# First mixer: two latent projections and the query projection interleaved with the gate projections

## The chip, the cores and the metric

The kernel runs on one core of a Trainium2 chip as one launch. The metric is the device time of that launch in microseconds (us); lower is better. Engines are named as in the profile: PE is TensorE (matmuls), PEld its weight loads, DVE is VectorE, ACT is ScalarE, POOL is GpSimd, SP issues the weight transfers.

## The reference, cut to what matters

Three blocks of a transformer (one hybrid block, then two layers with other mixers) run over 256 tokens of width 1024 in float32. The change lies in the mixer of the first block. With `h` the normalised input (256 x 1024):

```
z = h @ w_in                       # split: q_lat 256, c_kv 128 + k_pe 32, qb 512, kb 128, vb 128, gate_a 1024, gate_b 1024
cq   = rmsnorm(q_lat);  qa  = cq   @ w_qb    # 8 heads x (64 + 32), rope on the 32
c_kv = rmsnorm(c_kv);   kva = c_kv @ w_kvb   # 8 heads x (64 keys + 64 values)
oa = softmax(qa . [ka, rope(k_pe)]) va       # attention A, 8 heads
ob = softmax(rope(norm(qb)) . rope(norm(kb))) vb   # attention B, 8 query heads on 2 key heads
x += (sigmoid(gate_a) * (oa @ w_oa) + sigmoid(gate_b) * (ob @ w_ob)) @ w_o
```

So attention A needs the three short products of `cq` and `c_kv` (here: the latent projections), attention B does not, and the gates are needed only behind both.

## The kernel before, in words

**Tiles.** Activations lie transposed, features on the 128 partitions and the 256 tokens along the free dimension. Each operand is split in a high and a low part, and a product is three matmuls (`mm3`, L323 to L326: high weights times high and low activations, low weights times high ones). `gemm_a` (L328) makes two 128-column tiles of an output per PSUM bank of the tag `acc`, of which there are three, used in turn; `gemm_b` (L367) keeps tokens as rows and takes two of these banks. An `acc` bank is free again once DVE or ACT has read it.

**Weights.** All weights come through one stream, in the order in which they are used, 128 x 1024 floats per chunk. `Stream.prep` (L135) lets ACT make the rounded high part (L140), `Stream.low` (L145) lets DVE make the low part one chunk behind (L149), and this orders the next transfer on SP (L131). Eight 128-column pieces use up one chunk.

**Order.** Nothing is reordered by a planner: each engine runs its instructions in the order in which the Python code emits them. The emission is a round robin written out by hand (`Sched`): a projection is a generator that yields once per 128-column piece, that is per three matmuls; this is a **step** below. After each step every side task counts down and emits its next part when its count is over. Step 0 is here the first step after the query projection of attention B. `done` of a `gemm_a` tile pair is called as the next step begins, so the read of its bank stands in the queues ahead of that step's side tasks.

**The stretch in question.** Before: steps 0 to 3 are `kn` (4 pieces of w_kvb, keys of A, two banks, each read by two ACT copies, L861), steps 4 and 5 are `va` (gemm_b, one 512-column piece, matmuls at L374 to L376, banks read by ACT L864 and DVE L865), steps 6 to 21 are the query projection (w_qb, 8 tiles of 2 pieces, four banks, each read by a DVE multiplication with the rope table, L873), and steps 22 to 149 are the eight gate pairs (16 pieces each; a bank is read by DVE L887 and then ACT L888). Behind step 149, `drain` emits what attention still has, and then `gemm_merge` (matmuls of `oh`, `ol`) begins, first with the output of attention A.

Side tasks in this stretch, by their counts in the code: keys of B are transposed and scaled after step 16 (L711, DVE L713, ACT L714) and their low part made after step 19 (L716); a bias table for a much later mixer is made after step 19 (PE L546, ACT L548, an ACT-issued write to DRAM L549 and an ACT-issued broadcast L550 that reads it back); `attn1` (L766) takes B as soon as its keys and queries are there, in both kernels after step 20, and then moves one head every 6 steps: scores (PE L400 for B, L777 for A, bank tag `wk`, three banks), row maximum (DVE L791), exponential (ACT L797), transposes (PE L804, DVE L806), product with the values (PE L816). Head 8, the first of A, waits for the flag `qa`, which `ev_qa` sets after the fourth query bank:

```
while not all(z in st for z in need):
    yield 1
pr[i] = soft(*units[i])
```

Five steps after the last product of a half, `final` transposes the outputs (PE L831) and splits them into `oh` (ACT L406) and `ol` (DVE L407).

Of the kernel before, what the change touches and what calls it, by code (L numbers as in the profile page):

```python
# [217 lines left out]
def build(ctx, tc, nc, aps, total, stop=None):  # L218
# [22 lines left out]
    sc = Sched()  # L241
# [46 lines left out]
    def C(name, r=slice(0, P)):  # L288
        o, w = CST[name]
        if o >= NC1:  # L290
            return rope[0][r, o - NC1:o - NC1 + w]
        return cst[r, o:o + w]
# [18 lines left out]
    def t512():  # L311
        return tmp.tile([P, 512], F32, name="t512", bufs=7)
# [4 lines left out]
    def v2(ap):  # L317
        return ap.rearrange("p (a b) -> p a b", a=2)

    def bc(ap, n):  # L320
        return ap[:, None, :].to_broadcast([ap.shape[0], n, ap.shape[1]])

    def mm3(o, ah, al, bh, bl, start, stop_, joint=False):  # L323
        PE.matmul(o, ah, bh, start=start, stop=False, skip_group_check=joint)  # L324
        PE.matmul(o, ah, bl, start=False, stop=False, skip_group_check=joint)  # L325
        PE.matmul(o, al, bh, start=False, stop=stop_, skip_group_check=joint)  # L326

    def gemm_a(n, K, piece, rhs, done, M=P, lead=0, width=2, order=None, ready=None, joint=False):  # L328

        order = order or list(range(K))

        def part(t, ps, j, k0, k1):
            m = M(t) if callable(M) else M
            for k in order[k0:k1]:
                while ready and not ready(k):
                    yield
                wh, wl = W.get(piece(t, k), m)
                xh, xl = rhs(k)  # L340
                mm3(ps[:m, j * T:(j + 1) * T], wh, wl, xh, xl, k == order[0] and not (joint and j), k == order[-1], joint)
                yield

        i = 0
        if lead:
            banks = [(t, accb()) for t in range(0, 2 * width, 2)]
            i = 2 * width
            cuts = (0,) + (lead if isinstance(lead, tuple) else (lead,)) + (K,)
            for k0, k1 in zip(cuts, cuts[1:]):
                for t, ps in banks:  # L350
                    for j in range(1 + joint):
                        yield from part(t + j, ps, j, k0, k1)
                    if joint and k1 == K:
                        done(t // 2, ps)
            for t, ps in banks:
                if not joint:
                    yield from part(t + 1, ps, 1, 0, K)
                    done(t // 2, ps)
            joint = False
        while i < n:  # L360
            ps = accb()
            for j in range(min(2, n - i)):
                yield from part(i + j, ps, j, 0, K)
            done(i // 2, ps)
            i += 2

    def gemm_b(N, K, piece, lhs, done, tail=0, each=None):  # L367

        o = accb(), accb()

        def step(k, b, w):
            xh, xl = lhs(k)
            s = slice(b * P, (b + 1) * P)
            PE.matmul(o[b][:, :N], xh[:, s], w[0], start=(k == 0), stop=False)  # L374
            PE.matmul(o[b][:, :N], xl[:, s], w[0], start=False, stop=False)  # L375
            PE.matmul(o[b][:, :N], xh[:, s], w[1], start=False, stop=(k == K - 1))  # L376

        for k in range(K - tail):
            w = W.get(piece(k), N)
            for b in range(2):  # L380
                step(k, b, w)
                yield
        w = [W.get(piece(k), N) for k in range(K - tail, K)]
        for b in range(2):
            for j in range(tail):
                step(K - tail + j, b, w[j])
                yield
            if each:
                each(b, o[b])
        if done:  # L390
            done(o)
# [10 lines left out]
    def rhs_of(h, l):  # L402
        return lambda k: (h[:, k], l[:, k])
# [80 lines left out]
    hrhs = rhs_of(hx, lx)  # L484
# [5 lines left out]
    def later(n, fn):  # L490
        def g():
            yield n
            fn()
        sc.side(g())

    def idx(a, n):
        return list(range(a, a + n))
# [76 lines left out]
    ckh = mp.tile([P, T], F32R, name="ckh")  # L574
    ckl = mp.tile([P, T], F32R, name="ckl")
    cqh = mp.tile([P, 2, T], F32R, name="cqh")
    cql = mp.tile([P, 2, T], F32R, name="cql")
# [20 lines left out]
    def w_in_piece(tiles):  # L598
        return lambda t, k: ("w_in", k, tiles[t])
# [263 lines left out]
    def ev_va(p):  # L863
        S_.copy(vA[:, 0], p[0])  # L864
        V.tensor_copy(vA[:, 1], p[1])  # L865

    def qa_cols(h):
        b = h * 96
        return idx(b, 64) + idx(b + 64, 32) + idx(b + 80, 16) + idx(b + 64, 16)

    def ev_qa(i, ps):
        def go():
            V.tensor_tensor(QA[:, 2 * i:2 * i + 2], v2(ps), bc(C("tq"), 2), op=OP.mult)  # L873
            if i == 3:
                later(4, lambda: st.update(qa=True))
        sc.push(go)

    def latents():
        yield from gemm_a(4, 1, lambda t, k: ("w_kvb", 0, idx(t * 256, 64) + idx(t * 256 + 128, 64)), lambda k: (ckh, ckl), ev_kn)
        yield from gemm_b(512, 1, lambda k: ("w_kvb", 0, [h * 128 + 64 + j for h in range(8) for j in range(64)]),  # L880
                          lambda k: (ckh, ckl), lambda p: sc.push(lambda: ev_va(p)))
        yield from gemm_a(8, 2, lambda t, k: ("w_qb", k, qa_cols(t)), rhs_of(cqh, cql), ev_qa)

    def ev_gate(i, ps):
        def go():
            t = t512()
            V.tensor_tensor(v2(t), v2(ps), bc(n1.row, 2), op=OP.mult)  # L887
            S_.activation(sg[:, 2 * i:2 * i + 2], v2(t), AF.Tanh, scale=0.5)  # L888
        sc.push(go)

    gt = [idx(IN["ga"] + 128 * i, 128) for i in range(16)]

    sc.run(latents())
    sc.run(gemm_a(16, 8, w_in_piece(gt), hrhs, ev_gate))
    sc.flush()
    sc.drain(lambda: "o11" in st)

# [911 lines left out]
def make(arr, total, stop=None):  # L1809
    import concourse.bacc as bacc  # L1810

    nc = bacc.Bacc("TRN2", target_bir_lowering=False, num_devices=1, dynamic_dma_scratch_size=4096)
    aps = {n: nc.dram_tensor(n, v.shape, mybir.dt.from_np(v.dtype), kind="ExternalInput").ap() for n, v in arr.items()}
    aps["w"] = nc.dram_tensor("w", (total * P,), F32, kind="ExternalInput").ap()
    aps["out"] = nc.dram_tensor("out", (P, KD, T) if stop else (T, D), F32, kind="ExternalOutput").ap()
    with tile.TileContext(nc) as tc, ExitStack() as ctx:
        W = build(ctx, tc, nc, aps, total, stop)
    return nc, W
# [11 lines left out]
```

## Time and profile before

| | us |
|---|---|
| three runs, median | 1387.05 |
| lowest and highest of them | 1381.07, 1394.16 |
| profiled execution, its own time | 1386.93 |
| its span from first to last instruction | 1385.2 |
| PE busy in the span | 1360.4 (98%) |
| DVE busy | 909.1 (66%) |
| ACT busy | 689.0 (50%) |

The stretch from step 0 to step 149 lies at 40.6 to 141.8 us of the span. [...] In the chain of work that ended last PE holds 93% of the span and DVE 3%.

### The profile page before, as it was taken

How to read it: one execution, taken by the hardware profiler on the slowest of the kernel's cores; microseconds unless marked ns; L12 is line 12 of the kernel's file. 1: busy time of each engine (PE TensorE's matmuls, PEld its weight loads, DVE VectorE, ACT ScalarE, POOL GpSimd, SP SyncE). 2: the span in 40 equal slices, each digit the busy share in tenths (PEclk: the TensorE clock that was granted, in tenths of full speed). 3: DMA queues.
4: the chain of work that ended last, by engine and by line, in shares of the span. 5: the costliest groups of instructions: out<-in, count | busy, mean ns of one | idle time of the engine just before them, and what ended most of it. 6: DMA issues, size and time to landing. Idle time of an engine off the chain costs nothing.

```text
span 1385.2 us, 27163 instructions
## 1 busy us (share of the span) xinstructions
PE 1360.4 (98%) x11342; PEld 1333.0 (96%) x11342; DVE 909.1 (66%) x1254; ACT 689.0 (50%) x970; POOL 103.1 (7%) x108
## 2 busy tenths in 40 slices
PE   9899999999999999999999999999999999999998
PEld 8799999999999999997999999999999988999987
DVE  6866776656687665675865555655656777776553
ACT  6554465544554544453554444444444364544442
POOL 2300000000040000010000000000000271000001
PEclk9899999999999999999999999999999999999999
DMA  8533555665646656552455555555555532555552
GB/s 279 187 127 97 190 191 188 198 198 183 198 155 218 192 185 207 191 180 66 153 192 189 185 186 189 173 187 189 190 194 186 196 107 92 167 191 191 189 177 84
DMA packets 69642, 243.61 MB, mean 176 GB/s; under 512 B 7877, under 2 KB 11365, under 8 KB 69392
## 3 DMA queue, kind: packets, MB, share of 16 engines
q1 hardware_dynamic: 66096, 234.52, 51.6%
q10 hardware_dynamic: 2992, 5.99, 1.3%
q8 instruction: 89, 1.46, 0.4%
q0 software_dynamic: 432, 1.37, 0.3%
q14 instruction: 33, 0.27, 0.1%
HBM read 240.78 MB, written 4.22 MB: 177 GB/s over the span
## 4 chain that ended last, share of the span: by engine, by line
PE 93%; DVE 3%; issue 1%; DMA 1%; ACT 1%; POOL 1%; SPq 0%; POOLq 0%; DVEq 0%; ACTq 0%
PE acc L324 27%; PE acc L326 26%; PE acc L325 26%; PE acc L374 2%; PE acc L376 2%; PE acc L375 2%; PE pv L816 1%; PE wk L400 1%; DVE wlo L149 1%; DMA wraw<-w 1%; DVE iacc L1621 1%; PE wk L1212 1%; PE wk L804 1%; PE wk L777 0%; POOL rs_y L415 0%
## 5 line engine op out<-in xcount | busy, mean ns | idle before, releaser
L149 DVE TENSOR_TENSOR wlo<-wraw,whi 128x1024 fp32r<-128x1024 f32 (+2 forms) x442 | 533.2, 1220 | 248.5 <-PE acc L326 187.9
L140 ACT CAST whi<-wraw 128x1024 fp32r<-128x1024 f32 (+1 forms) x448 | 462.1, 1038 | 362.4 <-PE acc L325 261.5
L324 PE MATMUL acc<-hx,whi 128*128 128x256 f32 x2184 | 621.9, 285 | 0.2 <-ACT hx L410 0.2
L325 PE MATMUL acc<-lx,whi 128*128 128x256 f32 x2184 | 610.5, 280 | 1.4 <-DVE lx L411 1.4
L326 PE MATMUL acc<-hx,wlo 128*128 128x256 f32 x2184 | 610.7, 280 | 0.4 <-DVE wlo L149 0.4
L325 PEld LDWEIGHTS acc<-lx,whi 128*128 128x128 f32 x2184 | 412.9, 189 | 2.1 <-DVE lx L411 1.7
L326 PEld LDWEIGHTS acc<-hx,wlo 128*128 128x128 f32 x2184 | 413.3, 189 | 0.9 <-DVE wlo L149 0.9
L324 PEld LDWEIGHTS acc<-hx,whi 128*128 128x128 f32 x2184 | 410.8, 188 | 3.0 <-issue 0.6
L324 PE MATMUL acc<-gh,whi 128*128 128x256 f32 x784 | 218.1, 278 | 0.0
L325 PE MATMUL acc<-gl,whi 128*128 128x256 f32 x784 | 218.1, 278 | 0.0
L326 PE MATMUL acc<-gh,wlo 128*128 128x256 f32 x784 | 218.1, 278 | 0.0
L326 PEld LDWEIGHTS acc<-gh,wlo 128*128 128x128 f32 x784 | 147.9, 189 | 0.0
L325 PEld LDWEIGHTS acc<-gl,whi 128*128 128x128 f32 x784 | 147.9, 189 | 0.0
L324 PEld LDWEIGHTS acc<-gh,whi 128*128 128x128 f32 x784 | 147.2, 188 | 0.0
L415 POOL TENSOR_TENSOR rs_y<-col,mhalf 128x2 f32<-128x2 f32 (+2 forms) x17 | 19.1, 1124 | 823.8 <-DVE col L443 757.2
L407 DVE TENSOR_TENSOR gl<-t,gh 128x512 fp32r<-128x512 f32 x60 | 41.5, 692 | 41.4 <-ACT gh L406 41.4
L406 ACT CAST gh<-t 128x512 fp32r<-128x512 f32 x60 | 37.3, 622 | 45.7 <-DVE t L1086 33.3
L410 ACT ACTIVATE hx<-x,gains 128x256 fp32r<-128x256 f32 x64 | 29.5, 502 | 54.9 <-DVE x L482 48.8
L324 PE MATMUL acc<-oh,whi 128*128 128x256 f32 x192 | 54.8, 285 | 0.0
L325 PE MATMUL acc<-ol,whi 128*128 128x256 f32 x192 | 53.6, 279 | 0.0
L326 PE MATMUL acc<-oh,wlo 128*128 128x256 f32 x192 | 53.6, 279 | 0.0
L1086 DVE TENSOR_TENSOR t<-t,acc 128x512 f32<-128x512 f32 x44 | 30.3, 689 | 32.4 <-ACT t L1084 26.8
(383 smaller groups left out, 1478.9 us busy)
## 6 DMA issues: line engine op xcount, KB each, us to landing
wraw<-w SPq DMA_DIRECT2D x439, 512.0 KB, 4.2
t5r<-t5u ACTq DMA_DIRECT2D x1, 3072.0 KB, 12.0
Bt<-t5r ACTq DMA_DIRECT2D x1, 2048.0 KB, 11.9
wraw<-w SPq DMA_DIRECT2D x7, 256.0 KB, 4.7
x<-xt SPq DMA_DIRECT2D x8, 128.0 KB, 4.2
rope<-cst SPq DMA_DIRECT2D x1, 640.0 KB, 7.5
gfin<-gfin POOLq DMA_DIRECT2D x1, 512.0 KB, 5.4
out<-xg ACTq DMA_DIRECT2D x2, 256.0 KB, 2.8
```

Source lines behind the costliest of these rows:

```text
L140: self.nc.scalar.copy(self.hi[c][:, :n], self.raw[c][:, :n])
L149: self.low_eng.tensor_tensor(self.lo[c][:, :n], self.raw[c][:, :n], self.hi[c][:, :n].bitcast(F32), op=OP.subtract)
L324: PE.matmul(o, ah, bh, start=start, stop=False, skip_group_check=joint)
L325: PE.matmul(o, ah, bl, start=False, stop=False, skip_group_check=joint)
L326: PE.matmul(o, al, bh, start=False, stop=stop_, skip_group_check=joint)
L374: PE.matmul(o[b][:, :N], xh[:, s], w[0], start=(k == 0), stop=False)
L375: PE.matmul(o[b][:, :N], xl[:, s], w[0], start=False, stop=False)
L376: PE.matmul(o[b][:, :N], xh[:, s], w[1], start=False, stop=(k == K - 1))
L406: S_.copy(hi, src)
L407: V.tensor_tensor(lo, src, hi.bitcast(F32), op=OP.subtract)
L410: S_.activation(hi, src, AF.Copy, scale=g)
L1086: V.tensor_tensor(u, s, ps, op=OP.mult)
```

## The change

The short projections no longer stand ahead of all gates. New order of steps: gate pair 0 (16 steps), `kn` (4), gate pair 1 (16), `va` (2), then gate pair 2 cut in halves: 8 steps, query bank 0 (4), 8 steps, query bank 1 (4); gate pair 3 likewise with query banks 2 and 3; then gate pairs 4 to 7. The pieces, their number and all evaluations stay the same; the weights are packed in the new order.

```
-    sc.run(latents())
-    sc.run(gemm_a(16, 8, w_in_piece(gt), hrhs, ev_gate))
+    def gate(i):
+        return gemm_a(2, 8, w_in_piece(gt[2 * i:2 * i + 2]), hrhs, lambda z, ps: ev_gate(i, ps))
+
+    def query(i):
+        return gemm_a(2, 2, lambda t, k: ("w_qb", k, qa_cols(2 * i + t)), rhs_of(cqh, cql), lambda z, ps: ev_qa(i, ps))
+
+    def gates_and_latents():
+
+        yield from gate(0)
+        yield from gemm_a(4, 1, lambda t, k: ("w_kvb", 0, idx(t * 256, 64) + idx(t * 256 + 128, 64)), lambda k: (ckh, ckl), ev_kn)
+        yield from gate(1)
+        yield from gemm_b(512, 1, lambda k: ("w_kvb", 0, [h * 128 + 64 + j for h in range(8) for j in range(64)]),
+                          lambda k: (ckh, ckl), lambda p: sc.push(lambda: ev_va(p)))
+        for i in (2, 3):
+            g = gate(i)
+            for _ in range(8):
+                next(g)
+                yield
+            yield from query(2 * i - 4)
+            yield from g
+            yield from query(2 * i - 3)
+        for i in range(4, 8):
+            yield from gate(i)
+
+    sc.run(gates_and_latents())
```

The removed function `latents()` held the same three calls (`kn`, `va`, and the query projection as one `gemm_a` of 8 tiles).

## Rows read from the trace of the kernel before

**Rows 1.** Page, busy time of the engines, share of the span, instructions.
```profile
PE 1360.4 (98%) x11342; PEld 1333.0 (96%) x11342; DVE 909.1 (66%) x1254; ACT 689.0 (50%) x970; POOL 103.1 (7%) x108
```

**Rows 2.** Stretch: length, busy us per engine, granted clock, DMA share, GB/s.
```profile
40.60:62.60 22.00, 16.38 (x102) 13.39 (x100) 18.73 (x44) 11.64 (x21) 7.89 (x6) 0.86 0.50 163
```

**Rows 3.** Timeline, PE: start us, us, line, operation, [idle before, what ended it].
```profile
40.60 0.28 PE L324 MATMUL acc<-ckh,whi 128*128 128x256 f32 x1
...
44.22 0.51 PE L374 MATMUL acc<-whi,ckh 128*128 128x512 f32 x1 [2.04 <-ACT t L678]
...
54.78 0.38 PE L324 MATMUL acc<-cqh,whi 128*128 128x256 f32 x1
...
58.16 0.39 PE L400 MATMUL wk<-KBl,QBh 64*128 64x256 f32 x2 [1.25 <-DVE KBl L716]
...
58.94 0.39 PE L324 MATMUL acc<-cqh,whi 128*128 128x256 f32 x1
...
62.60 0.58 PE L400 MATMUL wk<-KBh,QBh 64*128 64x256 f32 x1 [0.89 <-ACT prob L797]
```

**Rows 4.** Timeline of DVE in the same stretch and at the first gate read.
```profile
50.43 0.68 DVE L865 COPY vA<-acc 128x512 f32<-128x512 f32 x1
...
55.02 0.68 DVE L873 TENSOR_TENSOR QA<-acc,rope 128x512 f32<-128x512 f32 x1
55.62 0.41 DVE L713 TENSOR_TENSOR s<-s,wk 128x256 f32<-128x256 f32 x1
...
57.68 0.42 DVE L716 TENSOR_TENSOR KBl<-s,KBh 128x256 fp32r<-128x256 f32 x1
...
74.51 0.68 DVE L887 TENSOR_TENSOR t<-acc,row 128x512 f32<-128x512 f32 x1
```

**Rows 5.** Timeline of ACT in the same stretch (ACTq: transfers issued by ACT).
```profile
44.05 2.36 ACT L861 COPY KA<-acc 64x512 f32<-64x512 f32 x4
...
56.06 0.41 ACT L714 CAST KBh<-s 128x256 fp32r<-128x256 f32 x1 [3.98 <-DVE s L713]
56.38 1.04 ACT L140 CAST whi<-wraw 128x1024 fp32r<-128x1024 f32 x1
...
57.82 0.34 ACTq L549 DMA_DIRECT2D t5u<-t5s  x1
60.68 0.56 ACTq L550 DMA_DIRECT2D t5r<-t5u  x1
61.35 0.56 ACT L797 ACTIVATE prob<-wk,col,fB 128x256 f32<-128x256 f32 x1 [3.56 <-DVE col L793]
```

**Rows 6.** Timelines of PE, DVE and ACT behind the last product of attention A.
```profile
128.49 0.36 PE L324 MATMUL acc<-hx,whi 128*128 128x256 f32 x1
...
130.30 1.04 PE L831 MATMUL wk<-cst_sb,t 128*128 128x128 f32 x8
...
128.27 1.29 DVE L823 TENSOR_TENSOR t<-pv,col 128x512 f32<-128x512 f32 x2 [1.84 <-PE pv L816]
...
130.61 0.69 DVE L887 TENSOR_TENSOR t<-acc,row 128x512 f32<-128x512 f32 x1
132.47 1.29 DVE L407 TENSOR_TENSOR ol<-wk,oh 128x512 fp32r<-128x512 f32 x2 [1.17 <-ACT oh L406]
...
131.87 1.05 ACT L406 CAST oh<-wk 128x512 fp32r<-128x512 f32 x2
```

**Rows 7.** Stretches after or around four pauses of PE, columns as in Rows 2.
```profile
46.40:49.50 3.10, 3.03 (x14) 3.03 (x15) 2.68 (x6) 1.55 (x3) 3.02 (x3) 0.50 0.40 148
59.80:66.90 7.10, 6.21 (x33) 5.46 (x33) 2.53 (x7) 4.13 (x13) 0.00 (x0) 0.52 0.90 309
1107.60:1114.40 6.80, 5.59 (x12) 3.98 (x13) 6.46 (x27) 4.07 (x6) 4.54 (x2) 0.50 0.27 86
1154.00:1160.00 6.00, 4.09 (x36) 3.75 (x33) 4.31 (x7) 3.45 (x7) 0.79 (x2) 1.00 0.09 31
```

**Rows 8.** Timeline, PE: the pause ahead of the third stretch of Rows 7.
```profile
1107.64 0.79 PE L374 MATMUL acc<-whi,ch 128*128 128x512 f32 x1 [2.09 <-DVE t L1654]
```

More of the change, by code (lines that the diff above doesn't have):

```diff
@@ L876, in ev_qa @@
         sc.push(go)
[L878 to L882, printed above, removed]
     def ev_gate(i, ps):
```

## The prediction

> **What bounds the kernel now.** I read the busy shares first: PE is busy 98% of the span [rows 1], so only the places where it stands still or runs at a lower clock can give anything. Walking the span in stretches of 4 to 20 us, one such place lies where the change is: in the 22 us from 40.6 to 62.6 PE is busy for 16.4 us, at a mean granted clock of 0.86, while DVE is busy for 18.7 us [rows 2]. The timeline of PE shows the pauses one by one [rows 3]: 2.04 us before `va`, whose bank is still to be read by ACT; some 2.4 us around the first scores of attention B, for the high and then the low part of the keys (the second wait, 1.25 us, is in the row); 0.89 us for an exponential. Then I read DVE and ACT in order [rows 4, 5] and asked which of them holds PE. DVE holds it until 58.2: it runs without a gap, and the keys (L713 at 55.62, L716 at 57.68) come where they stand in its queue. ACT holds it until 62.6: its exponentials begin at 61.35, right behind the issue at 60.68 of the bias table's broadcast, which has to wait until the small write issued at 57.82 has landed. So PE's own order hardly sets the end of this stretch, and reordering the matmuls alone does not shorten it. Behind it PE runs full until step 149.
>
> **The change part by part.** Matmuls and bytes stay equal in number, SP's queue keeps its rate per matmul, and POOL's instructions and order do not change; what moves is where reads of banks stand in the queues of DVE and ACT, and which steps cover attention.
>
> *Step 20, removal and new wait.* The wait of 2.04 us before `va` goes: gate pair 0 takes a bank that was read long ago. But DVE is behind PE at step 0, and nothing emitted before step 0 changes; it is free for later work at 50.43, as now [rows 4]. From there to L713 it now runs the `va` copy, two query reads, two low parts and the small work of a query pair. After the change the three reads (3 x 0.60, the distance of the rows at 55.02 and 55.62) are not yet there, but the read of gate pair 0 (0.60, by L887's like duration) is, and the low parts are again two: their prep falls after 5 and 13 steps instead of 6 and 11. So L713 begins at 55.6 - 1.8 + 0.6 = 54.4. PE needs 20 x 0.35 us and some small matmuls for steps 0 to 19, so it is at step 20 before 50, and there it waits: gate pair 1 takes the third bank, which the same DVE queue gives back only at about 54.4. This is a new pause of some 4 to 5 us in place of the old ones. Then the scores: ACT's `ev_gate` stands ahead of L714, so KBh comes at about 55.4 and KBl at 55.9; the first head's scores end at 55.9 + 0.8 (58.16 to 58.94 in [rows 3]) = 56.7, which is 2.2 us earlier than now.
>
> *Step 24, the exponential.* That gain stops at ACT. Now L714 to the first exponential is 61.35 - 56.06 = 5.3 us. In the new order one weight cast moves behind it (minus 1.0, L140) and the four copies of `kn` (2.36 us in [rows 5]), which now are emitted around step 19, stand between, two of them behind the broadcast's issue. From L714 at 55.0: 55.0 + 5.3 - 1.0 + 2.4 = 61.7, so PE resumes at about 62.95 where it is 62.60 now: plus 0.35. Bounds: if the exponentials were not held there, PE would go on at about 59 (minus 3.6); if the small write lands later or a cast slips in, plus 2. I take the middle row chain, since each of its links is a row.
>
> [...]
>
> *Work not yet done.* At step 25 the old order has done `va`, which is worth four pieces in two steps; the new one has not. Two pieces are left over: plus 2 x 0.35 = 0.7 us.
>
> *Steps 36 to 86.* A bank is wanted soon after it is filled in three places (gate pair 2 after `va`, pairs 3 and 4 after four query steps, some 1.4 us). DVE's first gate read now starts at 74.51, 1.2 us behind PE, and takes 0.68 [rows 4]; so a pause of up to 0.5 us can come at each. I take 0.3 in all; bounds 0 and 2. The query reads (4 x 0.68) lie in steps without attention, where DVE has one low part (1.2 us) per 2.8 us of PE: covered.
>
> *The tail of attention A.* `qa` is set at step 25 now, before it is wanted at step 58. After the change the fourth query bank ends with step 85, the flag is set in step 89, and `attn1` sees it in step 90: everything of A moves by exactly 32 steps. Its last product moves from step 114 to 146, and the outputs' transposes, five steps later, fall behind step 149: the drain emits them at once, and the merge, which wants `oh` and `ol` first, follows. The queue order from that product on is the same as now, since gate reads and weight chunks repeat every 16 and 8 steps. So I lay PE's new order on [rows 6]: product ends at 128.49, three steps (1.05) to 129.6, transposes (1.04) to 130.6; `oh` is there at 131.87 + 1.05 = 132.9 and `ol` at 132.47 + 1.29 = 133.8. PE does one matmul in between: 3.1 us of pause, uncovered. Bounds: 1.6 (without the gate read and its tanh ahead of the split) and 4.3 (one more low part, 1.2).
>
> [...] Around 62.6 PE is at half in the old order until 66.9 [rows 7]; I take the same for the new one.
>
> [...]
>
> **Sum.** 0.35 + 0.7 + 0.3 + 3.1 + 2.0 = +6.4 us on the profiled execution's 1386.93 us; that lies 0.1 us under the median of the runs, so the median becomes 1393.5. The ends of the terms give -1.3 (-3.6 + 0.7 + 0 + 1.6 + 0) and +12 (2 + 0.7 + 2 + 4.3 + 3.1): 1386 to 1399.
>
> **Rivals.**
>
> *A clean front.* The exponentials come before the table's write and the `kn` copies hold ACT, PE goes on at 59 instead of 62.95 (-4.0) and has no stretch at half behind it (-3.1, half of 6.2 busy us). For it: ACT has idle time there (3.56 us before the exponential, [rows 5]). Against it: that idle time is the wait itself, in program order. 1393.5 - 7.1 = 1386.4, from 1383 if the tail's clock stays up too.
>
> *A covered tail.* The flag is seen some five steps earlier than I count, or the drain leaves PE other work. Then 3.1 and 2.0 go: 1388.4. Against it: 32 steps follow from the code, and there is no other work behind step 149.
>
> *Slower: the half clock stays on.* After pauses of 4 to 5 us at step 20 and again before 62.95, PE goes through the heads of B at 0.50 beyond 66.9. Each us of full-speed work done so costs 1 us more. For it: [rows 7], 0.50 over 6.8 us though PE was mostly busy. Against: the stretch at half from 59.8 ends at 66.9, 4.3 us behind its last pause. It decides from 7.5 us of such work on (13.9 less 6.4); with 9 us the time is 1402.
>
> **How the numbers follow.** What a measurement of this kernel can tell from no change is about 1%, 13.9 us. Forecast 0.63 (1386 to 1399, no change by that bound), clean front 0.20, covered tail 0.09, half clock 0.08. All but the last stay within 1%; I leave 0.02 for faster, as all pauses and all half-clock time of the old stretch together are about 10 us. Faster 0.02, same 0.90, slower 0.08. The range takes in the first three and leaves the last out: 1383 to 1400.
>
> **What would show it.** In the new profile: the wait of `va` gone; PE waiting 4 to 5 us on a gate read (L887's counterpart) near 50 to 54; the first exponentials near 61.7, behind the broadcast's issue; the transposes of A's output behind the last gate matmul, then about 2 us without PE, a wait on `ol`, and a clock under 1.00 in the merge. Wrong, if PE passes step 24 before 60, if A's transposes lie among gate matmuls, or if the stretch at 0.50 goes on past 72.

## The result and the profile after

The changed kernel takes 1394.42 us (median of 20 runs, 1385.58 to 1405.14) against 1386.74 us (20 runs, 1381.07 to 1394.16): a ratio of 1.0066, 95% interval 1.0045 to 1.0087. A later series gave 1.0087 (1.0054 to 1.0120). It is slower, by less than 1%. The profiled execution took 1390.20 us, span 1388.4: 3.3 us more than the profiled execution of before, where the medians differ by 7.7. Each profile is one execution of a kernel whose executions lie up to 20 us apart.

The waits of PE around the change, after (line; what it waited for; us, times, longest):

```profile
PE acc L324 <- DVE t L881: 4.8, 1, 4.8
PE acc L324 <- ACT oh L406: 2.3, 1, 2.3
PE wk L400 <- ACT prob L797: 0.9, 1, 0.9
PE acc L325 <- DVE ol L407: 0.4, 1, 0.4
```

The wait ahead of `va` and the waits for the keys [rows 3] are gone; one wait for the read of gate pair 0 (L881, formerly L887) has their place, and two waits at the start of the merge are new. The same on the timelines, PE first, then DVE, then ACT:

```profile
54.44 0.58 PE L324 MATMUL acc<-hx,whi 128*128 128x256 f32 x1 [4.78 <-DVE t L881]
55.40 0.58 PE L400 MATMUL wk<-KBh,QBh 64*128 64x256 f32 x2
...
61.51 0.38 PE L400 MATMUL wk<-KBh,QBh 64*128 64x256 f32 x1 [0.94 <-ACT prob L797]
...
138.72 1.04 PE L831 MATMUL wk<-cst_sb,t 128*128 128x128 f32 x8
142.07 0.45 PE L324 MATMUL acc<-oh,whi 128*128 128x256 f32 x1 [2.31 <-ACT oh L406]
142.91 0.58 PE L325 MATMUL acc<-ol,whi 128*128 128x256 f32 x1 [0.38 <-DVE ol L407]
```

```profile
50.31 2.35 DVE L149 TENSOR_TENSOR wlo<-wraw,whi 128x1024 fp32r<-128x1024 f32 x2
...
53.70 0.68 DVE L881 TENSOR_TENSOR t<-acc,row 128x512 f32<-128x512 f32 x1
54.30 0.41 DVE L713 TENSOR_TENSOR s<-s,wk 128x256 f32<-128x256 f32 x1
55.37 0.43 DVE L716 TENSOR_TENSOR KBl<-s,KBh 128x256 fp32r<-128x256 f32 x1 [0.66 <-ACT KBh L714]
```

```profile
54.42 0.63 ACT L882 ACTIVATE sg<-t 128x512 f32<-128x512 f32 x1 [2.45 <-DVE t L881]
54.95 0.39 ACT L714 CAST KBh<-s 128x256 fp32r<-128x256 f32 x1
55.25 1.17 ACT L861 COPY KA<-acc 64x512 f32<-64x512 f32 x2
56.44 0.47 ACT L548 COPY t5s<-wk 16x384 f32<-16x384 f32 x1
56.94 0.34 ACTq L549 DMA_DIRECT2D t5u<-t5s  x1
58.47 0.55 ACTq L550 DMA_DIRECT2D t5r<-t5u  x1
59.06 1.18 ACT L861 COPY KA<-acc 64x512 f32<-64x512 f32 x2 [2.15 <-DMA t5u<-t5s]
60.25 0.56 ACT L797 ACTIVATE prob<-wk,col,fB 128x256 f32<-128x256 f32 x1
```

Read against [rows 4] and [rows 5], these lines say: DVE reaches L713 1.3 us earlier than before, ACT's order around the bias table is the forecast one, and the first exponential comes 1.1 us earlier. Granted clock and busy times after, in the stretch of [rows 2], behind the first scores, and at the merge (stretch, length, busy us of PE, PEld, DVE, ACT, POOL, clock, DMA share, GB/s):

```profile
40.60:62.60 22.00, 16.27 (x114) 14.25 (x113) 16.49 (x41) 11.83 (x21) 7.78 (x6) 0.84 0.48 173
...
56.00:60.00 4.00, 4.00 (x22) 3.63 (x22) 3.09 (x10) 1.81 (x4) 0.00 (x0) 0.50 0.08 30
60.00:64.00 4.00, 2.88 (x24) 2.27 (x23) 1.00 (x3) 3.99 (x13) 0.00 (x0) 0.96 1.02 410
...
142.00:147.00 5.00, 4.55 (x25) 4.28 (x26) 2.08 (x3) 1.06 (x2) 0.00 (x0) 0.66 0.16 67
```

**Two markers** split the span: the last gate multiplication of the merge and the first SwiGLU activation of the first ffn (the second number of the first row and the first number of the second one), before and then after:

```profile
L917 DVE SCALAR_TENSOR_TENSOR t<-sg,acc x4: 681/682/683, 148.0 to 165.0; 128x512 f32<-128x512 f32 x4
...
L1084 ACT ACTIVATE t<-t x44: 632/632/634, 410.4 to 1317.2; 128x512 f32<-128x512 f32 x44
```

```profile
L934 DVE SCALAR_TENSOR_TENSOR t<-sg,acc x4: 676/677/681, 150.3 to 167.0; 128x512 f32<-128x512 f32 x4
...
L1101 ACT ACTIVATE t<-t x44: 631/632/634, 419.5 to 1320.3; 128x512 f32<-128x512 f32 x44
```

At the first marker the changed kernel is 2.0 us late, at the second 9.1, at the end 3.2. Most of the 7.1 us between the markers arises in w_up and w_down, which the change does not touch and in which neither profile lists a wait of PE (busy for 171.50 of the 171.50 us from 196.0 on before, for 178.20 of the 178.20 us from 196.5 on after). From the last matmuls of the norm ahead of w_up (L424) to the first of the norm behind w_down (L432) PE takes 171.6 us before and 178.3 after:

```profile
195.93 0.38 PE L424 MATMUL wk<-cst_sb,rs_y 128*128 128x128 f32 x2
...
367.54 0.50 PE L432 MATMUL wk<-cst_sb,ssq 128*128 128x1 f32 x4
```

```profile
196.43 0.38 PE L424 MATMUL wk<-cst_sb,rs_y 128*128 128x128 f32 x2
...
374.73 0.50 PE L432 MATMUL wk<-cst_sb,ssq 128*128 128x1 f32 x4
```

The matmuls themselves are farther apart, at a granted clock of 1.00 (in 249 to 254 us in both, with 47 matmuls before and 44 after). Twelve steps (36 matmuls) of w_up, before and after:

```profile
249.90 0.28 PE L324 MATMUL acc<-hx,whi 128*128 128x256 f32 x1
...
253.98 0.28 PE L324 MATMUL acc<-hx,whi 128*128 128x256 f32 x1
```

```profile
249.65 0.28 PE L324 MATMUL acc<-hx,whi 128*128 128x256 f32 x1
...
253.89 0.28 PE L324 MATMUL acc<-hx,whi 128*128 128x256 f32 x1
```

4.08 / 36 = 113.3 ns before, 4.24 / 36 = 117.8 ns after. Below these are the **short and the long spacing**. Both kernels show both, in stretches of up to some 200 us: before, the merge and w_o (142 to 192 us) run at the long and w_up at the short one; after it is the other way round. So time is lost here in a third way, beside the two that the prediction counts, pauses of PE and a lower granted clock: PE is busy, its granted clock is 1.00, and its matmuls are still 4% farther apart.

### The profile page after: what moved, and what is told of

It reads as the page before. It is cut to its first block, busy times and chain, and to the rows that moved or that the text cites. A ratio compares the mean times of both kernels' runs of the same rounds, so it can differ in the third digit from the quotient of the medians.

```text
span 1388.4 us, 27157 instructions
## 1 busy us (share of the span) xinstructions
PE 1357.6 (98%) x11342; PEld 1330.8 (96%) x11342; DVE 909.9 (66%) x1254; ACT 689.0 (50%) x970; POOL 101.0 (7%) x108
## 4 chain that ended last, share of the span: by engine, by line
PE 65%; issue 3%; DVE 2%; ACT 0%; POOL 0%; POOLq 0%; DVEq 0%; ACTq 0%
PE acc L324 18%; PE acc L326 18%; PE acc L325 18%; PE acc L374 2%; PE acc L376 2%; PE acc L375 2%; DVE iacc L1638 1%; PE wk L400 1%; PE wk L1229 1%; POOL rs_y L415 0%; PE pv L1241 0%; PE pv L1242 0%; DVE wlo L149 0%; PE pv L1240 0%; PE wk L1382 0%
## 6 DMA issues: line engine op xcount, KB each, us to landing
x<-xt SPq DMA_DIRECT2D x8, 128.0 KB, 4.3
```

## The experiments

Ratios are to the kernel before, measured beside it; in brackets the 95% interval. "Start to merge" is the time from the eight small matmuls at L691 ahead of step 0 (39.0 us before and after) to the first marker: 126.0 before, 128.0 after. The *front* is the part of it up to the first heads of attention B, the *tail* is the end of attention A at the start of the merge.

**The tail alone**, twice. The old order, `qa` set in step 89:

```
-                later(4, lambda: st.update(qa=True))
+                later(68, lambda: st.update(qa=True))
```

> The old order with one edit: the flag for attention A is set in step 89 as in the changed kernel, so all of A moves by 32 steps and nothing ahead of it does. Theory 'tail': PE waits 2.3 us for oh and 0.4 for ol at the start of the merge, runs it at half clock for about 3.5 us, and the last gate multiplication of the merge starts 4.4 us later than before (169.4 instead of 165.0 us); the whole kernel 4 to 5 us slower, ratio 1.003. Rival 'spacing': this local loss is swamped by the spacing of plain matmuls, 113.4 or 117.8 ns in stretches of 100 us and more, drawn anew at small matmuls of the norms; then the local marker moves as above but the totals lie anywhere within 8 us of before.

> A second execution, with more runs, of the old order with attention A moved by 32 steps. Theory 'tail': the wait for oh 2.3 and for ol 0.5 us again, half clock behind it, the stretch named above 128 to 131 us; ratio to before 1.004 to 1.008, as the changed kernel has, so the tail alone accounts for the change's loss. Rival 'front and tail add': ratio 1.003 here, half of the changed kernel's.

Measured 1.0063 (1.0028 to 1.0097) and 1.0057 (1.0027 to 1.0087). Start to merge 128.1 and 126.5. The waits in the second execution:

```profile
PE acc L324 <- ACT oh L406: 2.3, 1, 2.3
PE acc L374 <- ACT t L678: 1.8, 1, 1.8
PE wk L400 <- ACT KBh L714: 1.4, 1, 1.4
PE wk L400 <- DVE KBl L716: 1.2, 1, 1.2
PE acc L325 <- DVE ol L407: 0.5, 1, 0.5
```

The tail's two waits appear with all the old waits of the front, and the ratio is that of the whole change. What follows: moving attention A by 32 steps is enough for the loss. The ratio is twice the 1.003 expected of the first series.

The marker of the first execution was expected at 169.4 and came at 169.2, but its step 0 began 2.1 us later; freed of that the delay is 2.1 us, and 0.5 us in the second execution, where 2 to 5 were expected. These two delays are too small as the price of the tail, because the front, which this edit does not touch, was 2.0 us shorter in both executions than in the profile of before: from the matmuls at L691 to the transposes of the second head 26.9 us instead of 28.95. Nearly all of that is the clock behind the wait for the first exponential: the same 4 us held 25 matmuls at 0.55 before and 37 at 1.00 in the second execution (first row before, second row tail alone):

```profile
63.00:67.00 4.00, 4.00 (x25) 3.78 (x24) 1.13 (x3) 2.58 (x9) 0.00 (x0) 0.55 1.11 387
```

```profile
63.37:67.37 4.00, 4.00 (x37) 3.86 (x34) 3.17 (x5) 2.52 (x7) 0.00 (x0) 1.00 0.97 319
```

With these 2.0 us the tail itself cost 4.1 us up to the marker in the first execution, near the 4.4 expected, and 2.5 us in the second, where the pause cost no clock at all:

```profile
142.00:147.00 5.00, 4.34 (x35) 4.14 (x36) 2.21 (x3) 1.21 (x2) 0.00 (x0) 1.00 0.20 78
```

**The front alone**, twice. The changed kernel with the query banks right behind `va`, so that A is not moved:

```
-        for i in (2, 3):
-            g = gate(i)
...
-        for i in range(4, 8):
-            yield from gate(i)
+        for i in range(4):
+            yield from query(i)
+        for i in range(2, 8):
+            yield from gate(i)
```

> The changed kernel with the four query banks right behind va instead of between halves of gate pairs, so the flag for attention A is set in step 57 and A is not moved; the first 38 steps are as in the changed kernel. Theory 'tail': no wait on oh, no half clock in the merge; the last gate multiplication of the merge at 162 to 163 us (165.0 before, about 167 in the changed kernel); the whole kernel 4.4 us under the changed one and 2 under before, ratio to before 0.9985. Rival 'the front costs it': it stays as slow as the changed kernel, 1.005.

> A second execution, with more runs, of the kernel with the change's front (gate pair 0, kn, gate pair 1, va) and without its tail (query banks right behind va). Theory 'the front wins a little, the rest is the draw of the spacing': from the small matmuls ahead of step 0 to the last gate multiplication of the merge 125 to 126.5 us (125.3 in the first execution, 126.0 before, 128.0 in the changed kernel); the ratio of the first runs, 1.0033, falls toward 1.000. Rival 'the front costs': ratio 1.003 again, with that stretch at 127 us or more, by more time at half clock.

Measured 1.0033 (1.0009 to 1.0056), then, on another chip, 0.9990 (0.9969 to 1.0010): the two series of one kernel differ by 0.0043 and their intervals hardly touch, so an interval from one series is too narrow here. Start to merge 125.3 and 125.4, both 0.6 to 0.7 us under the profile of before: the front neither costs nor wins anything that the whole time shows. The gain of 2 to 3 us at the marker that was expected came out at 0.7.

Over all experiments the loss goes with the end of attention A and not with the front: the series in which A ends at the merge have ratios of 1.0050 to 1.0087 (1.0017 with the added statistic below), those in which it ends earlier 0.9983 to 1.0033.

**Who holds PE in the front.** The changed kernel with the bias table's task 100 steps later:

```
-        yield 100
+        yield 200
```

> The changed kernel with the bias table's task 100 steps later (step 119), so its copy, write and broadcast leave ACT's queue ahead of the first exponentials. Theory 'ACT holds PE until the exponentials': the first one begins at 58.2 us instead of 60.25 (row maximum ready at 58.1), PE's wait for it ends near 59.4 instead of 61.5; 2 us saved in the front, the tail as in the changed kernel. Rival 'DVE holds PE': nothing moves by more than 0.5 us.

```profile
55.80 1.77 ACT L861 COPY KA<-acc 64x512 f32<-64x512 f32 x3
58.28 0.56 ACT L797 ACTIVATE prob<-wk,col,fB 128x256 f32<-128x256 f32 x1 [0.71 <-DVE col L793]
```

The first exponential comes at 58.28, as expected, and no longer waits for ACT; PE goes on at 60.04 instead of 61.51, 1.5 us earlier and not 2, because now its own matmuls fill the time: 0.21 us apart from 57.56 to 59.70, where they are 0.12 apart from 61.55 on (it has no wait there). Ratio 1.0050 (1.0024 to 1.0077): the tail is still there.

**The spacing.** A second execution of the changed kernel, and three kernels with two tiny instructions added to the merge, whose results nothing reads (the same place in all):

> The changed kernel unaltered, a second execution with a profile. Theory 'hidden state': the pauses are the same to 0.3 us (4.8 to 5.3 us for the gate read, 2.3 for oh), the last gate multiplication of the merge starts at 166.5 to 170.5 us depending on the spacing in the gates, and the way from there to the first SwiGLU activation is either 245 to 246 us or 252 to 253 us and nothing between, by the spacing in w_up and w_down. Ratio to before 1.004 to 1.009. Rival 'one slow place': that way is 252.5 us again to 0.2 us, because the stage itself is slower.

```
             split(mh[:, s2], ml[:, s2], v2(a))
+            if i == 1:
+                q = pvb()
+                for b in range(2):
+                    PE.matmul(q[:, b:b + 1], ident, onecol(D), start=True, stop=True)
```

> The changed kernel with one more pair of tiny matmuls (128 x 1 outputs, like those of a norm's statistic, result unused) put between the second and third quarter of the merge, about 154 us. Theory 'hidden state': the spacing of plain matmuls is a state of PE that small matmuls step on and that holds until the next ones; the changed kernel comes out of the tail's pause at 113.4 ns and turns to 117.8 ns at the norm near 193 us. With one step more the rest of the merge goes to 117.8 (plus 1 us) and w_up and w_down, 196 to 410 us, to 113.4 (minus 7): the first SwiGLU activation of the first ffn comes 5 to 7 us earlier than in the changed kernel (419.5 us), near 413, total ratio to before about 1.000 instead of 1.0066. Rival 'position': the spacing belongs to the stage or its data; nothing moves by more than 1 us.

```
+                    PE.transpose(q[:, b * P:(b + 1) * P], onecol(D).to_broadcast([P, P]), ident)
```

> The changed kernel with two extra 128 x 128 transposes (like those of a norm's row) at the same place of the merge, result unused. Theory 'hidden state': they step the state on like the statistic does, so 117.8 ns behind them and 113.4 ns in w_up and w_down; first SwiGLU activation near 413 us instead of 419.5. Rival 'position': it stays at 419 to 420.

> The old kernel with the pair of tiny matmuls at the same place of the merge. Theory 'hidden state': the old kernel is at 117.8 ns in the merge and at 113.4 from the norm near 196 us on; with one step more w_up loses the fast spacing: first SwiGLU activation at 415 to 419 us instead of 410.4, total 5 to 8 us slower, ratio 1.005. Rival 'position': 410 to 411 and no difference.

Spacing in ns at a granted clock of 1.00, the median of the distances on the PE timeline, and the way from the first marker to the second:

| kernel | merge | behind the added pair | w_up and w_down | marker to marker, us | ratio |
|---|---|---|---|---|---|
| before | 117.8 | | 113.3 | 245.4 | 1 |
| changed, 1st | 113.3 | | 117.8 | 252.5 | 1.0066 (1.0045 to 1.0087) |
| changed, 2nd | 117.8 | | 113.3 | 247.7 | 1.0087 (1.0054 to 1.0120) |
| changed + statistic | 113.3 | 117.8 | 113.3 | 245.4 | 1.0017 (0.9992 to 1.0042) |
| changed + transposes | 117.8 | 113.3 | 117.8 | 252.8 | 1.0073 (1.0045 to 1.0102) |
| before + statistic | 117.8 | 117.8 | 113.3 | 245.5 | 0.9983 (0.9964 to 1.0001) |
| tail alone, 1st, 2nd | 113.3, 113.3 | | 117.8, 117.8 | 252.8, 250.6 | 1.0063, 1.0057 |
| front alone, 2nd | 117.8 | | 113.3 | 247.3 | 0.9990 |

The row of the second marker in the changed kernel with the statistic, beside that of after above:

```profile
L1105 ACT ACTIVATE t<-t x44: 632/632/635, 414.9 to 1323.4; 128x512 f32<-128x512 f32 x44
```

So behind the pair of tiny matmuls in the merge the short spacing (113.3 ns) gave way to the long one (117.8) for the rest of it and w_up, after the norm, is at the short one: the second marker comes 4.6 us earlier in spite of the pair's own cost and the slower rest of the merge, 7.1 us less on the way between the markers, 6.7 of them in w_up and w_down. Behind the pair of transposes the long spacing gave way to the short one in the merge, and w_up went to long. The rival "position" is out: the same stage runs at either spacing. But my rule was too simple: the statistic added to the old kernel changed nothing, where I had expected a loss of 5 to 8 us, and the transposes met the long spacing, not the short one, and gave the opposite of what I had written. In all fourteen profiles, a merge that ends at the short spacing is followed by w_up at the long one, and the reverse, and w_up and w_down together take 171.6 us (nine profiles) or 178.3 (five) and nothing between. On the longer way between the markers "nothing between" did not hold, 247.7 us in the changed kernel's second execution: a part of it, some 2 us behind 367 us, varies as well, and no run shows why. That this execution had the long spacing in the merge, the first the short one, shows that the spacing can differ between executions of one kernel.

**Faster versions.** The front's stalls were put down to DVE's backlog, so attention was started 18 steps later and gates put first:

```
-    sc.side(attn1(2))
+    sc.side(attn1(2), 38)
...
         yield from gate(0)
+        yield from gate(1)
         yield from gemm_a(4, 1, lambda t, k: ("w_kvb", 0, idx(t * 256, 64) + idx(t * 256 + 128, 64)), lambda k: (ckh, ckl), ev_kn)
-        yield from gate(1)
```

The query banks stand right behind `va` in all of them; in the second version `gate(2)` as well ahead of `kn`; in the third also the bias table 100 steps later.

> The changed kernel with three edits: gate pair 1 ahead of kn, the query banks right behind va, and attention started 18 steps later (the side task gets a delay of 38), so that DVE's backlog of 5 us at step 0 is worked off under gate matmuls. Theory 'backlog': the pauses of both kernels between 40 and 63 us (5.5 us idle and about 4.6 us lost at half clock before) go, A ends 13 steps ahead of the merge, the last gate multiplication of the merge starts at 155 to 157 us instead of 165.0; whole kernel 8 to 10 us under before, ratio 0.993. Rival 'spacing': the marker moves but the total lies within 8 us of that. Rival 'DVE bound': the pauses only move to the kn and va banks and the marker stays above 162.

> As the kernel with attention started 18 steps later, but with gate pairs 0, 1 and 2 ahead of kn and va, since there PE waited 5.8 us at va for the read of gate pair 1. Theory 'backlog': three banks of 16 steps each cover DVE's 5 us, PE waits less than 1.5 us between 40 and 75 us, no half clock; the last gate multiplication of the merge starts at 156 to 158 us (165.0 before), the whole kernel 7 to 9 us under before, ratio 0.9945. Rival 'DVE bound': a wait of 2 us or more at va's banks or at the first scores is left and the marker stays above 160.

> As the kernel with three gate pairs first and attention 18 steps later, with the bias table's task also 100 steps later, since there the table's write and broadcast held ACT for 3 us, and with it two weight casts, a gate read and the first exponentials (5.6 us of PE). Theory 'ACT's queue': the first exponentials begin within 2.5 us of the first scores, PE waits less than 2 us in all between 40 and 80 us, the last gate multiplication of the merge starts at 156 to 159 us (165.0 before), whole kernel 6 to 8 us under before, ratio 0.995. Rival 'DVE bound': a wait of 3 us or more is left at the first scores or at kn and va, and the marker stays above 161.

| version | wait of PE in the front | start to merge, us | ratio |
|---|---|---|---|
| first | 5.8 us at `va` | 124.2 | 1.0003 (0.9980 to 1.0027) |
| second | 5.6 us for an exponential, 1.5 at `kn` | 126.0 | 1.0009 (0.9985 to 1.0033) |
| third | 4.0 us for an exponential, 1.4 at `kn` | 124.2 | 1.0009 (0.9984 to 1.0035) |

None beats the kernel before. The pause only moved, each time to the next thing that DVE or ACT had not yet done. In the first two versions it is DVE's read of a gate bank or its row maximum that comes late, but DVE itself had stood still for 1.6 to 1.7 us, waiting for a weight cast, and ACT makes that cast after standing still for 2.5 us behind the table's write (here the first version):

```profile
58.02 1.99 ACT L140 CAST whi<-wraw 128x1024 fp32r<-128x1024 f32 x2 [2.47 <-DMA t5u<-t5s]
```

In the third version the table is out of the way and DVE itself is the cause, the row maximum (L791) stands behind a gate read and three low parts:

```profile
58.27 2.36 DVE L149 TENSOR_TENSOR wlo<-wraw,whi 128x1024 fp32r<-128x1024 f32 x2
60.54 0.68 DVE L881 TENSOR_TENSOR t<-acc,row 128x512 f32<-128x512 f32 x1
61.14 1.22 DVE L149 TENSOR_TENSOR wlo<-wraw,whi 128x1024 fp32r<-128x1024 f32 x1
62.27 0.68 DVE L791 TENSOR_REDUCE col<-wk 128x2 f32<-128x512 f32 x1
```

What the rival "DVE bound" named came in all three, a long wait left over and a marker above 162, 160 and 161 us (163.1, 166.7, 165.1); that DVE alone is the holder is shown for the third only.

## Why the prediction was right, and where it was not

The forecast was plus 6.4 us, 1393.5; measured 1394.42, plus 7.7. The direction and its main cause, the tail of attention A, are shown by the experiments. That the sum comes so close is in part luck: against the two profiles the front was put 3.5 us too dear (plus 1.35 forecast, 2.2 us shorter up to the merge measured), a term behind the tail was missing, and the profiled executions themselves differ by 3.3 us and not by 7.7. The bound of 1% for what a measurement can tell from no change was too wide: the intervals here reach 0.2 to 0.35% to either side, and two series of one kernel differ by 0.4%.

*Step 20.* Right: L713 at 54.30 (54.4 forecast), the pause 4.78 us (4 to 5), the scores' first matmul at 55.40.

*Step 24.* The mechanism is right and was confirmed by moving the table; its size is off. The exponential came at 60.25, not 61.7, because the small write let ACT go on 1.53 us after its issue (56.94 to 58.47) instead of 2.86 [rows 5]. The DMA engines were nearly idle then, a share of 0.08 in 56 to 60 us (row above); before, the same stretch had 0.56:

```profile
56.00:60.00 4.00, 2.23 (x20) 1.90 (x21) 3.70 (x13) 1.72 (x3) 0.83 (x1) 0.97 0.56 167
```

All fourteen profiles go the same way: 2.8 to 2.9 us in the four with the old front (share 0.48 to 0.64 in the 2.9 us from the issue on), 1.5 to 1.9 us in the ten others (share 0.03 to 0.26). That the quiet DMA engines are the reason was not tried by itself.

*The half clock behind 62.6.* Wrong as a fixed cost: I let it run to 66.9 as in [rows 7]. In the first execution the stretch at 0.50 was over near 60 (0.50 in 56 to 60, 0.96 in 60 to 64), ahead of a wait for the exponential that PE would have met all the same. Together with the earlier exponential this brings the first head's transposes to 63.55 us, where they were at 65.63 before and 65.98 by the forecast. In the second execution of the changed kernel the clock was 0.50 in 60 to 64 and 0.82 in 64 to 68, and start to merge took 129.4 us instead of 128.0. The old front varies as much, by the same cause: 0.55 in 63 to 67 before, 1.00 in the tail alone. From the matmuls at L691 to the last matmul ahead of the merge PE takes 100.5 to 102.9 us in the four profiles with the old front and 100.8 to 103.3 in the four with the changed order up to there. So the profiles show no difference between the fronts, and the 2.2 us between the first two are within what one kernel varies by.

*Steps 36 to 86.* No wait there; 0.3 us had been allowed.

*The tail.* Right: transposes behind the last gate matmul, 2.31 us for `oh` and 0.38 for `ol`, 2.7 in all against 3.1; the waits are 2.3 and 0.4 to 0.5 in all seven executions in which A ends at the merge.

*The clock behind it.* No run shows the 2.0 us that the sum takes, an estimate; in its place the stretch at 142 shows 0.66 over 5 us, that is 3.4 us at half and some 1.6 lost. Six of the seven executions with this pause show 0.66 to 0.70 in such a stretch, the second of the tail alone 1.00. The bounds in the sum's ends, 0 and 3.1, were right.

*What was missing.* The spacing. All seven profiles without the tail's pause have the long spacing in the merge and the short one in w_up (before, both of the front alone, the three versions, before + statistic). Of the seven with the pause, five come out of it at the short spacing, and the four of these without an added pair have w_up and w_down at the long one: minus 1.9 us in the merge and w_o (some 430 matmuls by 4.5 ns), plus 6.7 in w_up and w_down. The added statistic gave these 6.7 us back in its profile, and its series has a ratio of 1.0017 where the changed kernel has 1.0066; as two series of one kernel differ by 0.0043, that difference alone does not settle how much of the median is spacing, and the changed kernel's second series has the highest ratio, 1.0087, though its profile has the short spacing in w_up and w_down. Term by term, the profiles give a tail of 2.7 us of pause, 0 to 1.7 of clock and, in four of the five executions with the pause and no added pair, about 5 net of spacing. That is in reach of the 0.6% measured, an account and not a proof: the medians were not profiled, and what the spacing does behind 420 us is left out of it.

*Rivals.* The covered tail is refuted, the clean front came half true (0.96 in 60 to 64 in the first execution, but ACT did hold the exponentials, until 60.25), and the slow rival's condition, half clock beyond 66.9, was met in neither execution of the changed kernel (0.82 in 64 to 68 in the second); with the added transposes, whose front is the same, the 0.50 lasted a little over 1 us longer than that (0.50 in 64 to 68, 0.97 in 68 to 72).

**Open:** what sets the spacing, and whether the pause has a part in it (five of seven against none of seven is a count, not a mechanism); it is shown only that in two executions it changed at an added pair of instructions, 113.3 to 117.8 ns and 117.8 to 113.3. Behind 420 us the spacing varies in all kernels: from the second marker to the end of the span it is 974.8 us before, 968.9 after and 981.5 in the second version, with no relation to the change that these runs show.

## What to carry to other kernels

When a projection is moved, follow the flag that it sets to the last consumer: here three short products were moved by up to 64 steps, and a whole attention slid past the work that had covered its end. DVE's queue lags here at the start of the stretch (PE waits 4.78 us for its read of a gate bank in the changed kernel), and moving the matmuls moved the pause in all four orders tried (waits of 4.0 to 5.8 us) and did not remove it; that the lagging queue's work has to shrink instead was not tried. One profile of each kernel is not enough to price a stretch of 29 us: the same instructions took 2.0 us less in two other executions. And a whole-kernel time of a PE-bound kernel should be read together with the spacing of its matmuls: here 6.7 us, 0.5% of the time, lay in the spacing in w_up and w_down, far from the edit.

## What the runs showed of the hardware that was not expected

Equal matmuls (128 x 128 by 256 columns) at a granted clock of 1.00 ran 113.3 or 117.8 ns apart, for hundreds of matmuls on end. The spacing changed at small matmuls of another shape, at the norm ahead of w_up (117.8 to 113.3 before, 113.3 to 117.8 after) and at two of the three added pairs: 4.5 ns by some 1500 matmuls of w_up and w_down is 6.7 us. In the changed kernel with the statistic, some 330 matmuls ahead of a norm ran at 117.8 ns, and those of w_up behind it at 113.3. Two waits of 2.7 to 2.8 us together were followed by a granted clock of 0.66 to 0.70 over 5 us in six executions and of 1.00 in a seventh. The same 4 us of the old front ran at 0.55 in one execution and at 1.00 in another. And a 24 KB write to DRAM that ACT issued released its waiting queue after 1.5 to 1.9 us or after 2.8 to 2.9.
